# A written order on TensorE from the second query chunk to branch A, with attention handed out one step at a time

## The chip, the cores and the metric

The kernel runs on one core of a Trainium2 chip. The metric is the device time of one execution in microseconds (us). The median of three runs of the kernel before is 1961.41 us, the runs lie between 1960.43 and 1962.89 us.

## What is computed

The kernel is one decoder block on 256 tokens with 2048 channels. Two token mixers run beside each other, are merged with sigmoid gates, and a SwiGLU feed-forward network follows. The change touches mixer A (attention with three kinds of keys: compressed, selected blocks, window), the gate of mixer A and the matrix that takes mixer A's output. All of it is float32.

```
h = rms_norm(x); P = h @ W_in          # q | k,v for 3 branches | gates | GDN parts | merge gates mA, mB
o_A = attention(q, k, v, gates)        # 16 heads in 4 groups of 4; three softmaxes per head
o_B = gated_delta_net(...)
x   = x + (sigmoid(mA) * (o_A @ W_brA) + sigmoid(mB) * (o_B @ W_brB)) @ W_out
x   = x + (silu(h2 @ W_gate) * (h2 @ W_up)) @ W_down
```

## The kernel before

**Dense chunks.** Every projection is cut into chunks of 512 output columns. `chunk_tok` computes one chunk for both token tiles (two tiles of 128 tokens). The weights come in pairs of two blocks of 128 rows (`load_pair`): one DMA of 512 KB into `raw` (4 buffers), a copy on ScalarE that rounds it to the upper part `whi` (line 107), and a subtraction on VectorE that leaves the lower part `wlo` (line 108); each of these has 3 buffers. One pair feeds 12 matmuls of 512 columns: 2 blocks, 2 token tiles, and 3 products each (lines 122, 123, 124). A chunk with 2048 input rows has 8 pairs. It accumulates in two PSUM banks out of four (`psm`, tag `mm`), one per token tile, and its `evac` function then takes them.

**Side work.** `chunk_tok` is a generator that yields after each pair. `run` calls `pump` at each yield, and `pump` advances the generator at the head of the queue `side` by one step. Attention is such a generator: `attend(gi, t, ...)` for head group `gi` and token tile `t`. The two token tiles of one group are alternated by `zipped`, one step of each in turn. Small results use four other PSUM banks (`sps()`, tag `sd`).

**Attention.** `evac_q` normalizes a query chunk (`normed_T`: square, sum, power, multiplication into `nv`, which has two buffers) and transposes it on TensorE. `attend` then does, for each of four heads, the products with the keys, a maximum on VectorE (line 514) and the exponentials with their sums on ScalarE (line 517). Token tile 0 uses one bank per head, token tile 1 two. After the fourth head a factor per row is worked out (lines 552 to 556). Then the probabilities go segment by segment (three for token tile 0, five for token tile 1): a multiplication by the factor (line 580, or 564 for the compressed keys), four transposes (583, 572), a split into `ph` and `pl` on ScalarE and VectorE (176 and 177, or 573 and 574), and matmuls with the values (588 to 590, or 575). At the end the result is split into `oTA_hi` and `oTA_lo`.

**The order.** A planner puts the traced instructions of each engine into one fixed queue per engine: it walks through a modelled time and takes what is ready, earlier traced work first. Each engine then works through its queue in that order. The order of the trace is thus not the order on TensorE. Traced after the first query chunk are the chunks q1, q2, q3, the four chunks of merge gate A (`mA`), the first six pairs of each of the first two chunks of branch A (`run_pair(br[0], br[1], 2)`, which then drains the side work), and the rest of branch A. Branch A's blocks 12 to 15 need the output of the last head group. When the attention is through, its SBUF pool `nsa` is closed (`scr.__exit__`), and a pool `gdn` is opened on the same memory; `gdn_prep` of the second mixer then loads rows (`N`, `Q`, `eR`, from `grow_d`) by DMA from SyncE's queue and works on them with VectorE (lines 723 to 729) and ScalarE (731 to 737).

Of the kernel before, what the change touches and what calls it, by code (L numbers as in the profile page):

```python
# [2 lines left out]

# [17 lines left out]
KD = D // P  # L21
# [3 lines left out]
R = 4  # L25
# [7 lines left out]
C_Q = 0  # L33
# [5 lines left out]
C_MA = 13392  # L39
C_MB = 15440  # L40
# [3 lines left out]
def tile_hybrid_block(  # L44
# [22 lines left out]
    nc = tc.nc  # L67
    x = x[0]
    out = out[0]
    w_in = w_in[0]  # L70
    w_branch_a = w_branch_a[0]
# [17 lines left out]
    def nm(s):  # L89
        uid[0] += 1  # L90
        return f"{s}_{uid[0]}"
# [4 lines left out]
    def sps():  # L96
        return pss.tile([P, 512], F32, tag="sd", name=nm("sd"))
# [12 lines left out]
        )  # L110
        return hi, lo

    def chunk_tok(w, c0, width, kts, stat, evac):
        ps = [psm.tile([P, 512], F32, tag="mm", name=nm("mm")) for _ in range(NT)]
        for k0 in range(0, kts, 2):
            hi, lo = load_pair(w, k0, c0, width)
            for j in range(2):
                kt = k0 + j
                for t in range(NT):
                    sh, sl = stat(kt, t)  # L120
                    o = ps[t][:, :width]
                    nc.tensor.matmul(o, lhsT=sh, rhs=hi[:, j, :width], start=kt == 0, stop=False)  # L122
                    nc.tensor.matmul(o, lhsT=sh, rhs=lo[:, j, :width], start=False, stop=False)  # L123
                    nc.tensor.matmul(o, lhsT=sl, rhs=hi[:, j, :width], start=False, stop=kt == kts - 1)  # L124
            yield
        for t in range(NT):
            evac(t, ps[t])
        yield
# [19 lines left out]
    side = deque()  # L148

    def pump(n=1):  # L150
        for _ in range(n):
            if not side:
                return
            try:
                next(side[0])
            except StopIteration:
                side.popleft()

    def drain():
        while side:  # L160
            pump()

    def run(gen, n=1):
        for _ in gen:
            pump(n)

    def run_pair(ga, gb, n):

        for g in (ga, gb):
            for _ in range(6):  # L170
                next(g)
# [19 lines left out]
    ident = consts.tile([P, P], F32, name="ident")  # L191
# [44 lines left out]
    nsa = scr.__enter__()  # L236
# [151 lines left out]
        nc.scalar.activation(hi, src, AF.Copy, scale=gcol)  # L388
        nc.vector.scalar_tensor_tensor(lo, src, gcol, hi.bitcast(F32), ALU.mult, ALU.subtract)

    def normed_T(pst, hi, lo, gcol):

        sq = nsa.tile([P, 512], F32, tag="sq", name=nm("sq"), bufs=1)
        nc.scalar.activation(sq, pst, AF.Square)
        ss = nsa.tile([P, 4], F32, tag="ss", name=nm("ss"), bufs=4)
        nc.vector.tensor_reduce(ss, sq.rearrange("p (g d) -> p g d", g=4), AX.X, ALU.add)
        rs = nsa.tile([P, 4], F32, tag="rs", name=nm("rs"), bufs=4)
        rstd_of(ss, 1.0 / DH, EPS, rs)
        nv = nsa.tile([P, 512], F32, tag="nv", name=nm("nv"), bufs=2)
        nc.vector.tensor_tensor(  # L400
            nv.rearrange("p (g d) -> p g d", g=4),
            pst.rearrange("p (g d) -> p g d", g=4),
            rs.unsqueeze(2).to_broadcast([P, 4, P]),
            ALU.mult,
        )
        pt = sps()
        for i in range(4):
            nc.tensor.transpose(pt[:, i * P : (i + 1) * P], nv[:, i * P : (i + 1) * P], ident)
        gained(hi, lo, pt.rearrange("p (g d) -> p g d", g=4), gcol)
# [3 lines left out]
    def evac_kv(b, kind):  # L413
        def f(t, ps):
            if b == 0:
                tm = nsa.tile([P, 512], F32, tag="nv", name=nm("nv"), bufs=2)
                nc.scalar.activation(tm, ps, AF.Copy)
                if t == 0:
                    rawT[kind] = nsa.tile([P, G, S], F32, tag="rawT", name=nm("rawT"))
                pt = sps()  # L420
                for i in range(4):
                    nc.tensor.transpose(pt[:, i * P : (i + 1) * P], tm[:, i * P : (i + 1) * P], ident)
                nc.vector.tensor_copy(rawT[kind][:, :, t * P : (t + 1) * P], pt.rearrange("p (g c) -> p g c", g=4))
                if t == 1:
                    side.append(compress(kind))
            elif kind == 1:
                hilo(vh[b][:, t, :], vl[b][:, t, :], ps)
            else:
                o = KOFF[(b, t)]
                normed_T(ps, kTh[:, :, o : o + P], kTl[:, :, o : o + P], kg[:, b : b + 1])  # L430

        return f

# [56 lines left out]
    def evac_q(gi):  # L490
        both = {}

        def f(t, ps):
            qh = nsa.tile([P, R, P], F32R, tag="qh", name=nm("qh"), bufs=4)
            ql = nsa.tile([P, R, P], F32R, tag="ql", name=nm("ql"), bufs=4)
            normed_T(ps, qh, ql, qg)
            both[t] = attend(gi, t, qh, ql)
            if t == 1:
                side.append(zipped(both[0], both[1]))

        return f
# [2 lines left out]

        return bass.AP(tensor=pw.tensor, offset=pw.offset, ap=[list(pw.ap[0]), [144, 2], [1, 128]])

    def attend(gi, t, qh, ql):
        W = 272 if t == 0 else 528
        pb = nsa.tile([P, R, 528], F32, tag="pbuf", name=nm("pb"), bufs=2)
        nmx = nsa.tile([P, R, 3], F32, tag="nmx", name=nm("nmx"), bufs=2)  # L510
        sm = nsa.tile([P, R, 3], F32, tag="sm", name=nm("sm"), bufs=2)
# [45 lines left out]
            segs = [(0, 1, 0), (128, 2, 0), (256, 0, 0)]  # L557
        else:
            segs = [(0, 1, 1), (128, 1, 0), (256, 2, 0), (384, 0, 0), (400, 2, 1)]
        po = sps()  # L560
        for i, (c0, b, kt) in enumerate(segs):
            ph = nsa.tile([P, 512], F32R, tag="ph", name=nm("ph"), bufs=2)
            if b == 0:
                nc.vector.tensor_tensor(
                    cb.rearrange("p r (q c) -> p r q c", q=3)[:, :, :, :16],
                    pb[:, :, c0 : c0 + 16].unsqueeze(2).to_broadcast([P, R, 3, 16]),
                    f[:, :, 0].unsqueeze(2).unsqueeze(3).to_broadcast([P, R, 3, 16]),
                    ALU.mult,
                )
                pt = sps()  # L570
# [4 lines left out]
                nc.tensor.matmul(po, lhsT=vst[:, gi, :], rhs=ph[:96], start=i == 0, stop=i == len(segs) - 1)  # L575
                yield
                continue
            n = P
            seg = pb[:, :, c0 : c0 + n]
            nc.vector.tensor_tensor(seg, seg, f[:, :, b].unsqueeze(2).to_broadcast([P, R, n]), ALU.mult)  # L580
            pt = sps()
            for r in range(R):
                nc.tensor.transpose(pt[:n, r * P : (r + 1) * P], pb[:, r, c0 : c0 + n], ident)  # L583
            pl = nsa.tile([P, 512], F32R, tag="pl", name=nm("pl"), bufs=2)
            hilo(ph[:n], pl[:n], pt[:n])
            gs = slice(gi * P, (gi + 1) * P)
            wh, wl = vh[b][:, kt, gs], vl[b][:, kt, gs]
            nc.tensor.matmul(po, lhsT=wh, rhs=ph[:n], start=i == 0, stop=False)
            nc.tensor.matmul(po, lhsT=wh, rhs=pl[:n], start=False, stop=False)
            nc.tensor.matmul(po, lhsT=wl, rhs=ph[:n], start=False, stop=i == len(segs) - 1)  # L590
            yield
# [21 lines left out]
    side.append(narrow())  # L613
    for c in (5, 0, 1, 2, 4):
        run(chunk_tok(w_in, C_KV + c * 512, 512, KD, stat_h, evac_kv(c // 2, c % 2)), 1)
    for gi in range(4):
        run(chunk_tok(w_in, C_Q + gi * 512, 512, KD, stat_h, evac_q(gi)), 1)


    keep = {n: dram.tile([NT, P, D], F32, name=n, bufs=1) for n in ("mA_d", "mB_d", "brA_d")}  # L620
# [1 line left out]
    def evac_keep(n, c):  # L622
        def f(t, ps):
            st = stream.tile([P, 512], F32, tag="stg", name=nm("stg"), bufs=2)
            nc.scalar.activation(st, ps, AF.Copy)
            nc.sync.dma_start(keep[n][t, :, c * 512 : (c + 1) * 512], st)

        return f

    def chunk_m(n, c, r):  # L630
        run(chunk_tok(w_in, (C_MA if n == "mA_d" else C_MB) + c * 512, 512, KD, stat_h, evac_keep(n, c)), r)

    for c in range(4):
        chunk_m("mA_d", c, 1)

    def stat_of(hi, lo):
        def f(kt, t):
# [3 lines left out]
        return f  # L641

    stat_oa = stat_of(oTA_hi, oTA_lo)
    br = [chunk_tok(w_branch_a, c * 512, 512, KD, stat_oa, evac_keep("brA_d", c)) for c in range(4)]
    run_pair(br[0], br[1], 2)
    scr.__exit__(None, None, None)
    for g in br:
        run(g)
# [53 lines left out]
    for cg in range(4):  # L702
        for c in range(8):
            o = c * 32 + 8 * cg + c
# [434 lines left out]
```

## Time and profile before

| | before |
|---|---|
| median of 3 runs | 1961.41 us |
| the profiled execution's own time | 1961.53 us |
| its span, first to last instruction | 1959.8 us |
| TensorE busy | 1934.2 us (99%) |
| VectorE busy | 1157.1 us (59%) |
| ScalarE busy | 928.9 us (47%) |
| mean granted TensorE clock | 0.997 |

TensorE's matmuls overlap each other in the profile, so that a matmul of 512 columns is shown with some 0.39 us while the next one starts about 0.23 us after it. The busy share therefore hides small waits; starts of successive matmuls show them.

### The profile page before, as it was taken

The page shows a single profiled execution, that of the slowest core. Times are in us where ns is not written, and L with a number is a line of the kernel's source. Part 1 is how long each engine was busy: PE and PEld are TensorE (multiplying, and loading weights), DVE is VectorE, ACT ScalarE, POOL GpSimd, SP SyncE. Part 2 cuts the span into 40 slices and gives each one's busy share as a digit, 9 for nine tenths or more (in the row PEclk, how much of TensorE's full clock was granted, in tenths as well). Part 3 has the DMA queues.
Part 4 walks back from the last instruction along what each step waited for, and adds up shares of the span by engine and source line. Part 5 has one row for each costly group of instructions (what it writes and reads, how often), then busy time and mean ns, then how long its engine had stood idle before and what let it go on. Part 6 is the DMA issues. An engine that isn't in the chain of part 4 may idle for free.

```text
span 1959.8 us, 27239 instructions
## 1 busy us (share of the span) xinstructions
PE 1934.2 (99%) x10469; PEld 1651.3 (84%) x10469; DVE 1157.1 (59%) x1717; ACT 928.9 (47%) x1377; POOL 54.0 (3%) x98
## 2 busy tenths in 40 slices
PE   7999999999999999999999999999999999999999
PEld 6878888887998998999987788888888888888887
DVE  5555766665468677787774755555544544544443
ACT  5434555555454554654543544444444444443333
POOL 0001000001000000100100000000000000000000
PEclk9999999999999999999999999999999999999999
DMA  7566555547756666565564956666666666666664
GB/s 226 167 193 183 168 145 162 171 152 213 209 172 200 173 178 198 164 191 166 153 200 153 345 190 184 191 190 187 189 188 192 190 188 191 191 188 204 203 206 136
DMA packets 207845, 367.10 MB, mean 187 GB/s; under 512 B 25593, under 2 KB 34786, under 8 KB 207330
## 3 DMA queue, kind: packets, MB, share of 16 engines
q1 hardware_dynamic: 207682, 365.35, 62.5%
q8 instruction: 82, 1.34, 0.3%
q14 instruction: 49, 0.40, 0.1%
q10 hardware_dynamic: 32, 0.01, 0.0%
HBM read 355.76 MB, written 9.45 MB: 186 GB/s over the span
## 4 chain that ended last, share of the span: by engine, by line
PE 96%; DMA 2%; DVE 1%; ACT 0%; SPq 0%; issue 0%; POOL 0%; ACTq 0%; POOLq 0%; DVEq 0%
PE mm L123 24%; PE mm L124 24%; PE mm L122 24%; PE mm L141 4%; PE mm L143 4%; PE mm L142 4%; PE sd L183 1%; PE sd L689 1%; PE sd L452 1%; PE sd L769 1%; DMA raw<-in_w_branch_b_dram 1%; PE sd L583 1%; DMA raw<-in_w_branch_a_dram 0%; PE sd L269 0%; DMA xin<-in_x_dram 0%; DMA N<-grow_d 0%
## 5 line engine op out<-in xcount | busy, mean ns | idle before, releaser
L108 DVE TENSOR_TENSOR wlo<-raw,whi 128x1024 fp32r<-128x1024 f32 x632 | 774.1, 1226 | 650.5 <-ACT whi L107 648.6
L107 ACT ACTIVATE whi<-raw 128x1024 fp32r<-128x1024 f32 x632 | 669.5, 1060 | 810.6 <-PE mm L124 675.4
L123 PE MATMUL mm<-wlo,hT_hi 128*128 128x512 f32 x704 | 276.7, 393 | 0.0
L124 PE MATMUL mm<-whi,hT_lo 128*128 128x512 f32 x704 | 276.1, 392 | 0.0
L124 PE MATMUL mm<-whi,h2T_lo 128*128 128x512 f32 x704 | 274.0, 389 | 0.0
L123 PE MATMUL mm<-wlo,h2T_hi 128*128 128x512 f32 x704 | 273.9, 389 | 0.0
L122 PE MATMUL mm<-whi,hT_hi 128*128 128x512 f32 x704 | 260.3, 393 | 0.0
L122 PE MATMUL mm<-whi,h2T_hi 128*128 128x512 f32 x704 | 249.9, 390 | 0.0
L143 PE MATMUL mm<-hT_hi,wlo 128*128 128x256 f32 x768 | 218.4, 285 | 0.0
L141 PE MATMUL mm<-hT_hi,whi 128*128 128x256 f32 x768 | 218.4, 285 | 0.0
L142 PE MATMUL mm<-hT_lo,whi 128*128 128x256 f32 x768 | 218.3, 284 | 0.0
L123 PEld LDWEIGHTS mm<-wlo,hT_hi 128*128 128x128 f32 x704 | 132.2, 188 | 27.6 <-issue 1.1
L124 PEld LDWEIGHTS mm<-whi,h2T_lo 128*128 128x128 f32 x704 | 132.1, 188 | 27.5
L124 PEld LDWEIGHTS mm<-whi,hT_lo 128*128 128x128 f32 x704 | 132.3, 188 | 27.2 <-issue 0.4
L122 PEld LDWEIGHTS mm<-whi,h2T_hi 128*128 128x128 f32 x704 | 132.2, 188 | 27.1
L123 PEld LDWEIGHTS mm<-wlo,h2T_hi 128*128 128x128 f32 x704 | 132.2, 188 | 27.1
L122 PEld LDWEIGHTS mm<-whi,hT_hi 128*128 128x128 f32 x704 | 132.1, 188 | 26.4 <-issue 0.2
L141 PEld LDWEIGHTS mm<-hT_hi,whi 128*128 128x128 f32 x768 | 147.2, 192 | 0.6
L142 PEld LDWEIGHTS mm<-hT_lo,whi 128*128 128x128 f32 x768 | 147.2, 192 | 0.2
L143 PEld LDWEIGHTS mm<-hT_hi,wlo 128*128 128x128 f32 x768 | 146.9, 192 | 0.4
L124 PE MATMUL mm<-whi,act 128*128 128x512 f32 x352 | 136.9, 389 | 0.0
L123 PE MATMUL mm<-wlo,act 128*128 128x512 f32 x352 | 136.9, 389 | 0.0
(292 smaller groups left out, 2244.7 us busy)
## 6 DMA issues: line engine op xcount, KB each, us to landing
raw<-in_w_in_dram SPq DMA_DIRECT2D x272, 512.0 KB, 3.6
raw<-in_w_gate_dram SPq DMA_DIRECT2D x88, 512.0 KB, 4.3
raw<-in_w_up_dram SPq DMA_DIRECT2D x88, 512.0 KB, 3.6
raw<-in_w_down_dram SPq DMA_DIRECT2D x88, 512.0 KB, 4.6
raw<-in_w_branch_a_dram SPq DMA_DIRECT2D x32, 512.0 KB, 4.6
raw<-in_w_branch_b_dram SPq DMA_DIRECT2D x32, 512.0 KB, 5.6
raw<-in_w_out_dram SPq DMA_DIRECT2D x32, 512.0 KB, 4.1
wc<-in_w_cmp_dram SPq DMA_DIRECT2D x16, 256.0 KB, 3.9
```

The source lines that it names most:

```text
L107: nc.scalar.activation(hi[:, :, :width], raw[:, :, :width], AF.Copy)
L108: nc.vector.tensor_tensor(lo[:, :, :width], raw[:, :, :width], hi[:, :, :width].bitcast(F32), ALU.subtract)
L122: nc.tensor.matmul(o, lhsT=sh, rhs=hi[:, j, :width], start=kt == 0, stop=False)
L123: nc.tensor.matmul(o, lhsT=sh, rhs=lo[:, j, :width], start=False, stop=False)
L124: nc.tensor.matmul(o, lhsT=sl, rhs=hi[:, j, :width], start=False, stop=kt == kts - 1)
L141: nc.tensor.matmul(o, lhsT=hi[:, j, ws], rhs=xh[:, kt, :], start=first, stop=False, skip_group_check=True)
L142: nc.tensor.matmul(o, lhsT=hi[:, j, ws], rhs=xl[:, kt, :], start=False, stop=False, skip_group_check=True)
L143: nc.tensor.matmul(o, lhsT=lo[:, j, ws], rhs=xh[:, kt, :], start=False, stop=last, skip_group_check=True)
L183: nc.tensor.transpose(pt[:, i * P : (i + 1) * P], s4, ident)
L452: nc.tensor.matmul(pc[:60, :P], lhsT=kp[:, l0 + l, :], rhs=wc[:, l, :], start=l0 + l == 0, stop=l0 + l == 31)
L583: nc.tensor.transpose(pt[:n, r * P : (r + 1) * P], pb[:, r, c0 : c0 + n], ident)
L689: nc.tensor.transpose(pt[:, i * P : (i + 1) * P], src(i), ident)
```

## The change

`attend` now begins with the transposes of its own query (`turned`), which makes one step more; `evac` of a query chunk only normalizes (`normed`). In the second half of `attend` the segments are shifted against each other: a step issues the value matmuls of the segment before (`weigh(i - 1)`), then the transposes and the split of this one (`turn(i)`), then the multiplication for the next one (`scale(i + 1)`). `chunk_tok` can yield twice per pair (`fine`). The chunks q1 to q3, mA 0 to 3 and the first twelve half pairs of branch A's first two chunks are traced under `tc.manual_schedule` for TensorE, which keeps TensorE's instructions in the order in which they are traced; the queues of the other engines are still the planner's. `spread` hands out 0.62 attention steps per yield.

```diff
-    def chunk_tok(w, c0, width, kts, stat, evac):
+    def chunk_tok(w, c0, width, kts, stat, evac, fine=False):
...
                     nc.tensor.matmul(o, lhsT=sl, rhs=hi[:, j, :width], start=False, stop=kt == kts - 1)
+                if fine and j == 0:
+                    yield
             yield
...
-    def normed_T(pst, hi, lo, gcol):
+    def normed(pst):
...
+        return nv
+
+    def turned(nv, hi, lo, gcol):
+
         pt = sps()
...
         def f(t, ps):
-            qh = nsa.tile([P, R, P], F32R, tag="qh", name=nm("qh"), bufs=4)
-            ql = nsa.tile([P, R, P], F32R, tag="ql", name=nm("ql"), bufs=4)
-            normed_T(ps, qh, ql, qg)
-            both[t] = attend(gi, t, qh, ql)
+            both[t] = attend(gi, t, normed(ps))
...
-    def attend(gi, t, qh, ql):
-        W = 272 if t == 0 else 528
+    def attend(gi, t, nv):
+        qh = nsa.tile([P, R, P], F32R, tag="qh", name=nm("qh"), bufs=4)
+        ql = nsa.tile([P, R, P], F32R, tag="ql", name=nm("ql"), bufs=4)
+        turned(nv, qh, ql, qg)
+        yield
...
+        def turn(i):
+            c0, b, kt = segs[i]
+            pt = sps()
+            ph = nsa.tile([P, 512], F32R, tag="ph", name=nm("ph"), bufs=2)
...
+            hilo(ph, pl, pt)
+            return ph, pl
+
+        def weigh(i, ph, pl):
...
+        scale(0)
+        got = None
+        for i in range(n + 1):
+            if i:
+                if i == 1:
+                    po = sps()
+                weigh(i - 1, *got)
+            if i < n:
+                got = turn(i)
+                if i + 1 < n:
+                    scale(i + 1)
+                yield
...
-    for gi in range(4):
-        run(chunk_tok(w_in, C_Q + gi * 512, 512, KD, stat_h, evac_q(gi)), 1)
+    run(chunk_tok(w_in, C_Q, 512, KD, stat_h, evac_q(0)), 1)
...
-    for c in range(4):
-        chunk_m("mA_d", c, 1)
...
-    br = [chunk_tok(w_branch_a, c * 512, 512, KD, stat_oa, evac_keep("brA_d", c)) for c in range(4)]
-    run_pair(br[0], br[1], 2)
+    br = [chunk_tok(w_branch_a, c * 512, 512, KD, stat_oa, evac_keep("brA_d", c), fine=True) for c in range(4)]
+
+    def spread(gens, share):
+
+        due = 0.0
+        for g in gens:
+            for _ in g:
+                due += share
+                while due >= 1.0:
+                    pump()
+                    due -= 1.0
+
+    assert len(side) == 1
+    with tc.manual_schedule(engines={mybir.EngineType.PE}):
+        spread([chunk_tok(w_in, C_Q + gi * 512, 512, KD, stat_h, evac_q(gi), fine=True) for gi in (1, 2, 3)], 0.62)
+        spread([gen_m("mA_d", c, True) for c in range(4)], 0.62)
+        spread([islice(g, 12) for g in (br[0], br[1])], 0.62)
+        drain()
     scr.__exit__(None, None, None)
     for g in br:
         run(g)
```

## Rows read from the trace of the kernel before

**Rows 1.** The page: engine totals, and the two weight-splitting groups.
```profile
PE 1934.2 (99%) x10469; PEld 1651.3 (84%) x10469; DVE 1157.1 (59%) x1717; ACT 928.9 (47%) x1377; POOL 54.0 (3%) x98
...
L108 DVE TENSOR_TENSOR wlo<-raw,whi 128x1024 fp32r<-128x1024 f32 x632 | 774.1, 1226 | 650.5 <-ACT whi L107 648.6
L107 ACT ACTIVATE whi<-raw 128x1024 fp32r<-128x1024 f32 x632 | 669.5, 1060 | 810.6 <-PE mm L124 675.4
```

**Rows 2.** Windows: length, busy us (count) of PE, PEld, DVE, ACT, POOL; clock, DMA.
```profile
211.00:448.00 237.00, 237.00 (x1208) 197.00 (x1207) 156.27 (x268) 137.14 (x317) 6.05 (x6) 1.00 0.53 156
448.00:480.00 32.00, 28.05 (x111) 20.75 (x109) 19.75 (x47) 16.89 (x24) 6.72 (x38) 0.95 0.82 215
480.00:512.00 32.00, 32.00 (x146) 26.62 (x145) 14.71 (x12) 14.07 (x17) 0.00 (x0) 1.00 0.75 229
```

**Rows 3.** Timeline of TensorE, 185 to 320 us: start, duration, engine, line, operation.
```profile
221.63 0.39 PE L123 MATMUL mm<-wlo,hT_hi 128*128 128x512 f32 x1
...
224.35 0.39 PE L123 MATMUL mm<-wlo,hT_hi 128*128 128x512 f32 x1
224.58 0.28 PE L521 MATMUL sd<-kTh,qh 128*128 128x256 f32 x1
...
225.48 0.38 PE L521 MATMUL sd<-kTh,qh 128*128 128x272 f32 x1
...
225.98 0.37 PE L521 MATMUL sd<-kTh,qh 128*128 128x256 f32 x1
```

**Rows 4.** Waits of TensorE, 440 to 480 us: total, times, longest.
```profile
PE mm L123 <- DVE wlo L108: 2.5, 2, 2.3
...
PE mm L122 <- ACT oTA_hi L176: 0.7, 1, 0.7
```

**Rows 5.** Timeline of all engines, 443 to 481 us; in brackets idle time, releaser.
```profile
453.55 0.40 PE L590 MATMUL sd<-ph,vl 128*128 128x512 f32 x1
...
454.06 0.32 POOL L695 MEMSET p<- 128x256 f32 x1 [161.80 <-PE sd L590]
...
454.63 0.51 PE L122 MATMUL mm<-whi,oTA_hi 128*128 128x512 f32 x1 [0.69 <-ACT oTA_hi L176]
...
457.76 0.20 ACT L736 ACTIVATE esc<-esc 128x4 f32<-128x4 f32 x1 [3.18 <-DVE esc L723]
...
460.39 0.73 PE L122 MATMUL mm<-whi,oTA_hi 128*128 128x512 f32 x2 [0.69 <-ACT whi L107]
...
463.40 0.68 PE L123 MATMUL mm<-wlo,oTA_hi 128*128 128x512 f32 x1 [2.28 <-DVE wlo L108]
...
463.94 0.63 ACT L737 ACTIVATE eR<-eR 128x512 f32<-128x512 f32 x1 [3.61 <-DMA eR<-grow_d]
...
464.48 1.04 ACT L107 ACTIVATE whi<-raw 128x1024 fp32r<-128x1024 f32 x1
...
466.44 0.63 PE L122 MATMUL mm<-whi,oTA_hi 128*128 128x512 f32 x1
```

**Rows 6.** Timeline of all engines, 416 to 426.5 us.
```profile
416.94 0.29 PE L529 MATMUL sd<-mask,identb 128*128 128x272 bf16 x1
...
419.94 1.29 DVE L580 TENSOR_TENSOR pb<-pb,fac 128x512 f32<-128x512 f32 x2
...
422.24 0.24 PE L543 MATMUL sd<-mask,identb 128*128 128x144 bf16 x1
...
424.76 1.90 DVE L580 TENSOR_TENSOR pb<-pb,fac 128x512 f32<-128x512 f32 x3
```

**Rows 7.** Timeline of all engines, 436.5 to 439 us.
```profile
436.76 0.60 PE L583 MATMUL sd<-ident,pb 128*128 128x128 f32 x4
...
438.03 0.69 DVE L177 TENSOR_TENSOR pl<-sd,ph 128x512 fp32r<-128x512 f32 x1 [1.73 <-ACT ph L176]
```

**Rows 8.** Timeline of all engines, 386.9 to 390.6 us.
```profile
387.89 0.60 PE L583 MATMUL sd<-ident,pb 128*128 128x128 f32 x4
...
390.07 0.69 DVE L177 TENSOR_TENSOR pl<-sd,ph 128x512 fp32r<-128x512 f32 x1
```

More of the change, by code (lines that the diff above doesn't have):

```diff
@@ L2 @@
 from contextlib import ExitStack
+from itertools import islice
 import concourse.bass as bass
@@ L429, in f @@
                 o = KOFF[(b, t)]
-                normed_T(ps, kTh[:, :, o : o + P], kTl[:, :, o : o + P], kg[:, b : b + 1])
+                turned(normed(ps), kTh[:, :, o : o + P], kTl[:, :, o : o + P], kg[:, b : b + 1])
         return f
@@ L559, in attend, with scale @@
             segs = [(0, 1, 1), (128, 1, 0), (256, 2, 0), (384, 0, 0), (400, 2, 1)]
-        po = sps()
-        for i, (c0, b, kt) in enumerate(segs):
-            ph = nsa.tile([P, 512], F32R, tag="ph", name=nm("ph"), bufs=2)
+        n = len(segs)
+        def scale(i):
+            c0, b, kt = segs[i]
             if b == 0:
@@ L569, in attend @@
                 )
-                pt = sps()
+            else:
+                seg = pb[:, :, c0 : c0 + P]
+                nc.vector.tensor_tensor(seg, seg, f[:, :, b].unsqueeze(2).to_broadcast([P, R, P]), ALU.mult)
+        def turn(i):
+            c0, b, kt = segs[i]
+            pt = sps()
+            ph = nsa.tile([P, 512], F32R, tag="ph", name=nm("ph"), bufs=2)
+            if b == 0:
                 for r in range(R):
@@ L574, in attend @@
                 nc.vector.tensor_tensor(ph[32:64], pt[32:64], ph[32:64].bitcast(F32), ALU.subtract)
[L575 to L581, printed above, removed]
+                return ph, None
             for r in range(R):
-                nc.tensor.transpose(pt[:n, r * P : (r + 1) * P], pb[:, r, c0 : c0 + n], ident)
+                nc.tensor.transpose(pt[:, r * P : (r + 1) * P], pb[:, r, c0 : c0 + P], ident)
             pl = nsa.tile([P, 512], F32R, tag="pl", name=nm("pl"), bufs=2)
-            hilo(ph[:n], pl[:n], pt[:n])
+            hilo(ph, pl, pt)
+            return ph, pl
+        def weigh(i, ph, pl):
+            c0, b, kt = segs[i]
+            if b == 0:
+                nc.tensor.matmul(po, lhsT=vst[:, gi, :], rhs=ph[:96], start=i == 0, stop=i == n - 1)
+                return
             gs = slice(gi * P, (gi + 1) * P)
             wh, wl = vh[b][:, kt, gs], vl[b][:, kt, gs]
[L588 to L591, printed above, removed]
+            nc.tensor.matmul(po, lhsT=wh, rhs=ph, start=i == 0, stop=False)
+            nc.tensor.matmul(po, lhsT=wh, rhs=pl, start=False, stop=False)
+            nc.tensor.matmul(po, lhsT=wl, rhs=ph, start=False, stop=i == n - 1)
+        scale(0)
[10 more added lines that the diff above has]
+                yield
         ts = slice(t * P, (t + 1) * P)
@@ L628, in evac_keep, with gen_m @@
         return f
+    def gen_m(n, c, fine=False):
+        return chunk_tok(w_in, (C_MA if n == "mA_d" else C_MB) + c * 512, 512, KD, stat_h, evac_keep(n, c), fine)
     def chunk_m(n, c, r):
-        run(chunk_tok(w_in, (C_MA if n == "mA_d" else C_MB) + c * 512, 512, KD, stat_h, evac_keep(n, c)), r)
-    for c in range(4):
-        chunk_m("mA_d", c, 1)
+        run(gen_m(n, c), r)
     def stat_of(hi, lo):
```

## The prediction

> **What bounds the kernel now.** The page comes first: TensorE is busy for 99% of the span, the other engines far less [rows 1], so only time in which TensorE does not take its next matmul can be won. Busy time cannot show that, because matmuls overlap in it. So the pitch comes next: between two starts of line 123 lie 12 matmuls and 2.72 us, 0.2267 us each [rows 3]. Then the windows over the stretch that the change touches, from the end of the first query chunk (211 us) to the end of branch A (512 us). From 211 to 448 the busy time of TensorE fills the window [rows 2], and the view of its waits between 205 and 440 us has no row. From 480 to 512 it is full again. Only 448 to 480 is not: 28.05 us busy, clock 0.95, 111 matmuls, four of which are transposes that began before 448 and end there. The other 107 have 512 columns and need 107 x 0.2267 = 24.3 us. They took 32 us less some 0.2 us for the transposes' end and 0.1 us for the change of kind. **About 7.4 us are lost there**, and nowhere else in the stretch.
>
> What they are is in the waits and the timeline. First, the tail of the attention: the last value matmul starts at 453.55, the first matmul that needs its result at 454.63 [rows 5], 1.08 us instead of 0.23; the planner had nothing else ready. Second, a starved weight path. When the attention ends, the second mixer's pool opens (GpSimd's first memset waits for that very matmul), and its preparation gets into the queues of ScalarE and VectorE between the splits of the weights. ScalarE stands 3.18 us before `esc` and 3.61 us before `eR`, both waiting in the end for a DMA, while `whi` stands behind; TensorE gets weights at 460.39 and, after 2.28 us without work, at 463.40 [rows 4, 5]. Third, the clock: from 463.40 to 466.44 lie seven matmuls at 0.434 us, against 0.2267; the granted clock of the window, 0.95, shows the fall to the lower level [rows 2, 5]. About eight matmuls at 0.2 us too much are 1.65 us. The first part is about 0.9 us, with small delays before it 1.4; the rest, some 6 us, is the starved path and its clock.
>
> **The change, part by part.** All matmuls, transposes, copies and DMAs are issued as often as before; the work on TensorE is the same, so the sum is what the 7.4 us become, and which new waits the written order makes.
>
> *Where the attention ends.* A half step is 6 matmuls, 1.36 us. A chunk gives 16 half steps and 17 yields. A head group needs 20 steps (9 for token tile 0, 11 for token tile 1) and one empty call, four groups 84, of which one is done before the written part. The three calls of `spread` may hand out 31, 42 and 14 (0.62 of 51, 68 and 24 yields). So the last step of the attention falls on half step 3 of branch A's second chunk, and nine half steps (12.2 us) of other work still stand before the first matmul that needs the last group. The first loss, 1.4 us, is gone.
>
> *The starved path (cost D).* The pool still opens when the last step is through, and the same preparation, with its ten DMAs, still enters both queues. What changes is the lead. Before, TensorE's prepared weights at 454.63 lasted for some 4.5 us, 1.7 pairs, because the blocks that waited for the last group held all three weight buffers. With dense work at hand the three buffers are full, two to three pairs, 2.5 in the mean. That is 0.8 pairs, 2.2 us, more against a starvation of 6 us; and if no single wait is as long as 2.28 us, the 1.65 us of the clock fall away too. I take 6.0 - 2.2 - 1.65 = **2.1 us** that remain, between 0 (the planner puts the splits first) and 4.2 (the clock falls again).
>
> *Splits that are one step old (cost A).* The value matmuls of a segment now stand at a fixed place, one step of their token tile later. While both tiles alternate, that is two steps, at least 4 us, and the split needs 1.36 us from the last transpose to the end of `pl` (437.36 to 438.72) [rows 7] or, with a weight split ahead on VectorE, 2.27 us (388.49 to 390.76) [rows 8]: covered. Token tile 1 has two steps more than tile 0; there its steps follow one another. I count the yields: of these eight places, four have two half steps between (2.72 us, covered) and four only one, 1.36 us. Each of the four waits 0 to 0.9 us; with 0.45 that is **1.8 us** (0 to 3.6). Nothing else can run on TensorE meanwhile.
>
> *The first transposes after the softmax (cost B).* They stand behind the maximum, three exponentials, the factor and `scale(0)`. In the trace this took 3.4 us from the end of the last mask matmul to the end of the first multiplication for token tile 0 (417.23 to 420.6) and 3.0 us for tile 1 (422.48 to 425.4) [rows 6]. With the key products of a step at 0.9 us for tile 1 and 0.5 us for tile 0 [rows 3], the written order leaves these gaps, counted in yields: tile 0: 5.0, 5.0, 3.6, 3.6 us for the four groups; tile 1: 3.2, 4.5, 3.2, 3.2 us (for the first, two half steps and the 0.45 us of tile 0's transposes). With a chain of 3.7 us, a little above the rows, as weight splits lie between, the waits are 0.2 + 1.4 = about **1.5 us**; at the rows' own 3.0 and 3.4 us they are nothing, and with one whole weight split more (1.06 us [rows 1], so a chain of up to 4.5 us) 3.9 us.
>
> *A bank (cost C).* `nv` has two buffers, and a query now stays in `nv` until its group's first step. The third chunk's normalization waits for the step of group 2 that comes one half step into the second mA chunk. Its two banks are thus not free when that chunk starts, and it must take those that the chunk before it has just filled, behind a copy of 128x512 (some 0.6 us for such a copy: in [rows 7] the one ahead of the subtraction lies between 437.36 and 438.03). Half of this lies under the other tile's matmuls: **0.5 us**, from 0 to 1.1.
>
> *The clock after short waits.* The rows show that about 0.85 us without a matmul at 454 us did not lower the clock (it fell only after the 2.28 us), so waits of the kind above cost their length and no more. The Trainium skill, page "TensorE: Matmul & The Clock Gate", section "A second HAM failure mode: psum-queue depth-cycling", says that small idle times between groups of matmuls can make the clock swing between its two levels; by that rule each wait would cost more than its length. The trace so far doesn't bear it out.
>
> Sum: 2.1 + 1.8 + 1.5 + 0.5 = 5.9 us of 7.4 us are given back: **-1.5 us**. The profiled execution took 1961.53 us (a span of 1959.8 and 1.7 us around it), 0.12 us over the median, so it is 1961.41 - 1.5 = **1959.9 us**.
>
> **The rivals.** 0.2% is 3.9 us, about what a measurement of this kernel can tell from no change.
> (1) *The covers hold.* The planner knows the written order, traces the attention's work ahead of the weights and fits it in; A and B come to 1 us together, D to 1, C to 0.3. Result -5.1 us, 1956.3. For it: VectorE and ScalarE are free for 34% and 42% of 211 to 448 us [rows 2], and TensorE had no wait there. Against it: that order was chosen by readiness.
> (2) *The other side: the preparation starves the weights as before.* If ScalarE's queue holds `whi` behind `eR` for the whole 10 us between 454.06 and 464.48 [rows 5], TensorE needs 3.7 pairs in that time and has 2.5 to 3; it waits some 2 to 3 us and loses the clock, 4.2 us, and a second round for the next group adds up to 2 more, so that only 1.4 us of the 7.4 are won. With A to C at their middle, 3.8, this is +2.4 us; the kernel is slower by over 0.2% once A to C exceed 5.3 us: at their upper ends (8.6) it is +7.2 us, 1968.6.
> (3) *The clock swings.* If each of about ten waits lowers the clock as at 463.40, that is 10 x 1.65 = 16 us, 1976. The page named above speaks for it, the pitch after 454 us against it.
> (4) *The change does nothing*: the planner's order is like the written one, with the same tail. The steps make this unlikely, as the tail moves by nine half steps.
>
> **How the numbers follow.** The forecast's case has 0.42, the covers that hold 0.33, the starved path 0.15, the clock 0.05, no effect 0.05. Of the forecast's case 0.04 may fall under -3.9 us; of the starved path's, a third (0.05) stays within 3.9 us. So faster is 0.33 + 0.04 = 0.37, same 0.38 + 0.05 + 0.05 = 0.48, slower 0.10 + 0.05 = 0.15. The likeliest case alone has 1957 to 1963. The range for 8 in 10 goes from 1954.4 (nearly all 7.4 us won) to 1966.5 (the second rival half way).
>
> **What would show it.** Right: no wait of TensorE for `oTA_hi`; the first memset of the second mixer's pool some 12 us before branch A's first matmul on block 12; short waits of the value matmuls at the end of a group; a wait for `whi` or `wlo` after the pool opens that is shorter than 2.28 us. Wrong: TensorE's waits for `scale` or `ph` sum to over 5 us, or the clock falls in several places; or the planner orders the second mixer and branch B differently, which this sum leaves out: branch B has a similar stretch that could move by some us either way.

## The result, and the profile after

The changed kernel takes 1983.99 us, the median of four runs (1981.6 to 1987.55), beside 1961.33 us before: a ratio of 1.0116 (95% interval 1.0102 to 1.013), so 22.7 us slower. The forecast was 1959.9 us, its range ended at 1966.5 us. The profiled execution took 1981.6 us with a span of 1979.9 us, 20.1 us over that of before; it is the fastest of the four, and what makes the median 2.4 us longer than it is in no trace.

All of the 20.1 us arise where the order was written. The last matmul of branch A starts at 510.95 us before and at 531.03 us after, 20.1 us later; the last of branch B then comes at 1155.46 us instead of 1135.37, the last of the feed-forward network at 1975.07 instead of 1955.00, still 20.1 us. TensorE's busy total, 1934.2 us in [rows 1], is now 1939.4 us, and its share fell from 99% to 98%.

The windows of the changed kernel, with the columns of [rows 2]. The stretch from 211 to 448 us, which was full, now has 11.5 us in which no matmul runs, and the one from 448 to 480 lost still more than before.

```profile
211.00:448.00 237.00, 225.50 (x1125) 184.83 (x1124) 150.18 (x260) 132.23 (x309) 6.53 (x6) 0.99 0.47 140
448.00:480.00 32.00, 26.53 (x109) 20.51 (x108) 17.89 (x46) 12.73 (x17) 4.33 (x37) 0.89 0.68 191
```

The waits of TensorE between 205 and 440 us, where before has no row at all. Line 593 is the transposes of a segment, line 580 the multiplication (`scale`) ahead of them, 415 the transposes of a query, 601 the value matmul of the compressed keys. The second row names `whi`, which the transposes don't read; by the program what they wait for there is `scale` as well.

```profile
PE sd L593 <- DVE pb L580: 8.4, 3, 4.1
PE sd L593 <- ACT whi L108: 1.9, 2, 1.2
PE sd L415 <- DVE nv L403: 1.4, 1, 1.4
PE sd L601 <- DVE ph L590: 1.2, 2, 0.6
PE sd L415 <- DVE ss L384: 1.0, 1, 1.0
```

And between 440 and 535 us, the answer to [rows 4]: no wait for `oTA_hi`, a longer one for `wlo`.

```profile
PE mm L124 <- DVE wlo L109: 4.9, 2, 4.4
PE sd L601 <- DVE ph L590: 0.6, 1, 0.6
```

Waits leave out the time in which a late matmul gets going, so the account is made from starts. From 200 us to branch A's last matmul, each distance between two starts is taken less the pitch of its kind (0.227 us for 512 columns, 0.109 to 0.125 for 128 to 272 columns, 0.04 for the mask products). Distances over it by 0.5 us are put down to the matmul that came late; 512-column pitches near 0.427 us, where the granted clock is 0.50, the lower of its two levels, to the clock. What is left over is the last row but one.

| lost on TensorE, us (places) | before | after |
|---|---|---|
| first transposes after the softmax (cost B) | 0 | 11.1 (5) |
| transposes of the first group's query | 0 | 2.7 (2) |
| value matmuls of the compressed keys (cost A) | 0 | 2.3 (3) |
| weights not ready (cost D) | 3.3 (2) | 5.2 (2) |
| the tail, for `oTA_hi` | 0.9 (1) | 0 |
| 512-column matmuls at the lower clock | 1.4 (7) | 4.2 (21) |
| all smaller distances | 8.0 | 9.2 |
| sum | 13.5 | 34.7 |

The sum rose by 21.2 us; the changed kernel came to this stretch 1.1 us earlier, which gives the 20.1 us.

What cost B looks like is seen in the timeline of head group 1, token tile 1 (TensorE, then VectorE, then ScalarE). The last product with the keys (its mask) ends at 297.07 us, the first transposes start at 305.08.

```profile
296.83 0.24 PE L550 MATMUL sd<-mask,identb 128*128 128x144 bf16 x1
...
301.32 0.39 PE L125 MATMUL mm<-whi,hT_lo 128*128 128x512 f32 x1
305.08 0.99 PE L593 MATMUL sd<-ident,pb 128*128 128x128 f32 x4 [3.37 <-DVE pb L580]
...
297.12 1.22 DVE L109 TENSOR_TENSOR wlo<-raw,whi 128x1024 fp32r<-128x1024 f32 x1
...
298.53 0.83 DVE L521 TENSOR_REDUCE nmx<-sd 128x1 f32<-128x256 f32 x3
299.27 0.68 DVE L399 TENSOR_REDUCE ss<-sq 128x4 f32<-128x512 f32 x1
299.87 1.22 DVE L109 TENSOR_TENSOR wlo<-raw,whi 128x1024 fp32r<-128x1024 f32 x1
301.00 0.68 DVE L180 TENSOR_TENSOR pl<-sd,ph 128x512 fp32r<-128x512 f32 x1
...
301.82 0.69 DVE L399 TENSOR_REDUCE ss<-sq 128x4 f32<-128x512 f32 x1
302.42 0.22 DVE L560 RECIPROCAL fac<-fac 128x12 f32<-128x12 f32 x1
302.83 1.23 DVE L109 TENSOR_TENSOR wlo<-raw,whi 128x1024 fp32r<-128x1024 f32 x1 [0.19 <-ACT whi L108]
...
304.24 1.89 DVE L580 TENSOR_TENSOR pb<-pb,fac 128x512 f32<-128x512 f32 x3
...
297.84 0.60 ACT L397 ACTIVATE sq<-mm 128x512 f32<-128x512 f32 x1 [1.82 <-PE mm L125]
...
300.03 0.47 ACT L524 ACTIVATE pb<-sd,nmx 128x256 f32<-128x256 f32 x1
...
301.18 0.61 ACT L397 ACTIVATE sq<-mm 128x512 f32<-128x512 f32 x1
```

The chain itself is the maximum (521), the exponentials (524), the factor (560) and `scale` (580). In VectorE's queue stand between and before them three weight splits, a split of another tile (180) and the sums of squares of the next query chunk (399), which ScalarE's squares (397) must bring first. VectorE is busy for all but 0.9 us of the time to the end of the first multiplication: TensorE is not waiting for one late result but for a queue to be worked off. From the last mask product to the end of the first multiplication are 7.9 us, instead of the 3.0 us that [rows 6] show for the last head group.

### The profile page after: what moved, and what is told of

Same layout as the page of the kernel before. It is cut to its first block, busy times and chain, and to the rows that moved or that the text cites. A ratio compares the mean times of both kernels' runs of the same rounds, so it can differ in the third digit from the quotient of the medians.

```text
span 1979.9 us, 27247 instructions
## 1 busy us (share of the span) xinstructions
PE 1939.4 (98%) x10469; PEld 1653.4 (84%) x10469; DVE 1159.0 (59%) x1717; ACT 932.1 (47%) x1377; POOL 53.3 (3%) x98
## 4 chain that ended last, share of the span: by engine, by line
PE 94%; DMA 2%; DVE 2%; ACT 1%; SPq 0%; issue 0%; POOL 0%; ACTq 0%; POOLq 0%; DVEq 0%
PE mm L124 24%; PE mm L123 24%; PE mm L125 24%; PE mm L144 4%; PE mm L146 4%; PE mm L145 4%; PE sd L186 1%; PE sd L734 1%; PE sd L459 1%; DMA Q<-grow_d 1%; PE sd L814 1%; DVE wlo L109 1%; DMA raw<-in_w_branch_b_dram 1%; ACT whi L108 1%; PE sd L593 1%; PE sd L272 0%
## 5 line engine op out<-in xcount | busy, mean ns | idle before, releaser
L123 PE MATMUL mm<-whi,hT_hi 128*128 128x512 f32 x704 | 268.4, 401 | 0.0
```

## The experiments

Theory 1: the time is lost in the written order's own waits. It has two forms: (1a) the chain to the first transposes is long where the next query chunk's normalization falls into it; (1b) it is long everywhere. The rival, theory 2, is the weight path that the second mixer's preparation starves. All ratios are to the kernel before, run in the same job.

**Planned order, same steps.** The written order is taken away, all else stays.

```diff
-    with tc.manual_schedule(engines={mybir.EngineType.PE}):
+    with ExitStack():
```


> The changed kernel with the same steps, the same half-pair yields and the same share of 0.62, but without the written order: the planner orders TensorE again. Theory 1 (the loss is TensorE standing in a fixed order before the first transposes after a softmax, whose chain sits in the queues of VectorE and ScalarE behind other work; 11.1 us of waits and some 3.6 us of lowered clock): these waits go, and the time falls from 1984 to between 1956 and 1964 us. Rival (the finer steps and the reordered segments themselves cost, by more changes of kind on TensorE and more side work per stretch, whoever orders TensorE): it stays at 1976 us or more.

1960.44 us, ratio 0.9994 (0.9984 to 1.0003). The finer steps, the shifted segments and the moved transposes cost nothing where the planner orders them; TensorE then waits only for weights (3.6 us). The whole loss belongs to the written order: theory 1.

**One step more between softmax and transposes**, and a share that keeps the end in place.

```diff
         scale(0)
+        yield
...
-        spread([gen_m("mA_d", c, True) for c in range(4)], 0.62)
+        spread([gen_m("mA_d", c, True) for c in range(4)], 0.70)
...
```


> The changed kernel with one more step (a yield) between the first multiplication by the factor and the first transposes, in both token tiles, and a share of 0.70 in place of 0.62 so that the eight more steps still fit before branch A's second half. Theory 1: the chain after the softmax gets two more turns, some 5 us, beside the 3.2 to 5 us it had, against chains of 4 to 8 us in the trace; the waits of the first transposes fall from 11.1 us to under 2 us and the two falls of the clock go: about 1984 - 13 = 1971 us. Rival (the chain is late because VectorE and ScalarE have too much to do in this stretch; a longer distance only moves the wait to the next step): 1980 us or more.

1972.88 us, 1.0054 (1.0039 to 1.0069): 11.1 us won; the share alone won 4.7 (next experiment). The waits of line 593 are gone altogether. The two longest of TensorE's waits between 205 and 535 us are now for weights, all after 449 us:

```profile
PE mm L123 <- ACT whi L108: 4.7, 1, 4.7
PE mm L124 <- DVE wlo L109: 4.7, 2, 3.0
```

**The share alone**, in all three calls, without the new step.

```diff
-        spread([gen_m("mA_d", c, True) for c in range(4)], 0.62)
+        spread([gen_m("mA_d", c, True) for c in range(4)], 0.70)
...
```


> The changed kernel with a share of 0.70 in place of 0.62 and nothing else. By counting yields, the first transposes of token tile 1 then no longer fall just behind the end of a query chunk in groups 0 and 1, but in the middle of a chunk, or before its end; every gap gets a little shorter (1.43 half steps a turn in place of 1.61). Theory 1a (the two long waits, 4.3 and 3.5 us, come from the normalization of the next query chunk, which stands inside the softmax chain on VectorE): they fall to some 1.5 us, and the clock no longer falls there: 1984 - 8 = 1976 us. Theory 1b (the chain is long anyway, the normalization is by chance beside it): shorter gaps make longer waits, 1984 to 1990 us.

1979.29 us, 1.0088 (1.0073 to 1.0103): neither form as forecast. The first long wait stays (3.2 us; the normalization still stands in that chain), the second falls to 0.96 us, and the waits of line 593 are 7.5 us in total. Which chains meet the normalization changes with the share; one of the two still did.

**Five steps ahead**, the share as it was.

```diff
+    pump(5)
     with tc.manual_schedule(engines={mybir.EngineType.PE}):
```


> The changed kernel in which five steps of the attention are issued ahead of the written part, so that all later steps fall eight half steps earlier in the chunks; gaps and share stay. The first transposes of groups 0 and 1 then fall into the middle of a query chunk, away from its normalization. Theory 1a (the normalization inside the softmax chain makes the two long waits): they fall from 4.1 and 3.4 to some 1.5 us, and the two falls of the clock go: 1984 to 1975 us. Theory 1b (the chain is as long anywhere): 1982 us or more.

1972.83 us, 1.006 (1.0047 to 1.0074). The attention runs ahead of the normalization, and only two waits of line 593 are left, 2.5 us in total, the longest 1.3. Head group 1, token tile 1 again:

```profile
285.61 0.24 PE L550 MATMUL sd<-mask,identb 128*128 128x144 bf16 x1
...
291.70 0.63 PE L593 MATMUL sd<-ident,pb 128*128 128x128 f32 x4 [1.24 <-ACT whi L108]
```

From mask product to the end of the first multiplication, the chain of token tile 1 takes 5.8, 5.7, 4.2 and 4.2 us here for the four groups, and 7.2, 7.9, 4.8 and 4.2 us in the changed kernel. TensorE's work in between is as long as before in group 1 (4.5 us), so there the shorter chain alone shortens the wait, from 3.37 to 1.24 us: 1a holds for the long waits. In group 0 the place gave one half step more as well (4.45 us of work instead of 3.1), so its wait fell for both reasons. But 1b is right in part: without any normalization in it the chain still takes 4.2 to 5.8 us, behind the weight splits and the subtraction of the other token tile.

**Rows not loaded.** `N`, `Q` and `eR` of the first two head groups are filled with a constant by GpSimd, so their decay factors are not the true ones.

```diff
+        if hg < 2:
+            for v in (st.N, st.Q, st.eR):
+                nc.gpsimd.memset(v, -3000.0)
+        else:
...
```


> The changed kernel in which the rows of the second mixer's first two head groups are not loaded by DMA but filled with a constant by GpSimd; that leaves out ten DMAs of these rows, and the decay factors of these groups are then not the true ones, while all the work on VectorE, ScalarE and TensorE stays. Theory 2 (the starvation of 466 to 479 us comes from ScalarE and VectorE waiting in order for these DMAs): about 7 us go, 1984 to 1977 us. Rival (the preparation's own work on the two engines starves the weight splits): at most 2 us go.

1979.61 us, 1.0083 (1.0066 to 1.01), 4.4 us won. Two waits for `wlo` are left, 1.76 and 1.82 us: VectorE's work on the rows still stands between the splits, and six of its instructions took 5.33 us beside GpSimd's filling, so the run is confounded. By starts the waits for weights fell from 5.2 to 3.9 us, and the fall of the clock behind them (1.6 us) is gone; how much of the rest is the filling stays open here.

**Preparation behind the splits**, in the kernel before and in the changed one. The VectorE and ScalarE work of `gdn_prep` is ordered behind the newest weight split; the ten loads stay where they were.

```diff
+    def behind(after, inst):
+        tc.add_manual_dep(
+            inst.ins, after.name,
+            mybir.DependencyInfo(mybir.DependencyClass.NoSync, mybir.DependencyReason.DATA),
+            reason="behind a weight pair",
+        )
...
-        nc.scalar.activation(st.N, st.N, AF.Exp, scale=-1.0)
+        behind(na, nc.scalar.activation(st.N, st.N, AF.Exp, scale=-1.0))
...
```


> The kernel before with one thing changed: the work of the second mixer's preparation on VectorE and ScalarE (the factors esc, N, Q, eR of a head group) is put behind the newest weight split traced ahead of it on the same engine, by an ordering edge without a semaphore; the loads stay where they are. Theory 2 (from 458 to 476 us TensorE starves because these instructions stand, waiting for their DMAs, in front of weight splits): the starvation and the lowered clock, some 6 us, go: 1961 to 1955 us. Rival (the splits are late because all three weight buffers were held by blocks that waited for the last head group): 0 to 2 us go.

> The changed kernel with the same edge for the preparation. Theory 2: the 7.3 us between 466 and 480 us go, 1984 to 1977 us. Rival (the preparation's place has nothing to do with it, the written order itself is late there): within 2 us of 1984.

Before: 1959.79 us, 0.9991 (0.9982 to 1.0), only 1.4 us won, at the edge of the noise. After: 1978.48 us, 1.009 (1.0076 to 1.0104), 5.5 us won in the median; the profiled execution, 1982.11 us, is the slowest of the four and shows no gain up to branch A's end. In the first, one wait of 4.5 us for `whi` takes the place of the shorter ones, with nothing of the preparation in the queues of ScalarE and VectorE; ScalarE stands there for 9.2 us before a copy that waits for an earlier store of branch A's result. Its stretch up to branch A's end is 1.7 us longer than in the kernel before. What it won lies later: 1.9 us between branch A's last matmul and branch B's first, 0.5 us within branch B.

**The written order mended**: the new step and the share 0.70, the preparation behind the splits, and the first group's first step three half steps after its query chunk.

```diff
-    run(chunk_tok(w_in, C_Q, 512, KD, stat_h, evac_q(0)), 1)
+    for i, _ in enumerate(chunk_tok(w_in, C_Q, 512, KD, stat_h, evac_q(0))):
+        if i < 8:
+            pump()
...
         scale(0)
+        yield
...
-    def spread(gens, share):
+    def spread(gens, share, due=0.0):
...
-        spread([gen_m("mA_d", c, True) for c in range(4)], 0.62)
+        spread([gen_m("mA_d", c, True) for c in range(4)], 0.70)
...
```


> The written order with what the runs so far point to: one more step between the softmax and the first transposes, a share of 0.70, the preparation's work behind the weight splits, and the first group's first step three half steps after its query chunk rather than at its end. If the waits found so far are all there is (11.1 + 3.6 for the first transposes and their clock, 7.3 for the preparation, 2.7 at the start): 1984 - 24 = 1960 us, the kernel before's time. If the written order costs elsewhere too: 1965 us or more.

1965.97 us, 1.0024 (1.0015 to 1.0034). 18 of 22.7 us are back, less than forecast; TensorE has one long wait, 5.5 us for `whi`, and the transposes at the start wait no more. Here the cause can be read, since VectorE and ScalarE are idle beside it. SyncE's queue and ScalarE in the timeline of this run:

```profile
447.55 1.71 SPq L102 DMA_DIRECT2D raw<-in_w_branch_a_dram  x1
449.31 1.98 SPq L778 DMA_DIRECT2D eR<-grow_d  x1
...
457.25 1.25 SPq L778 DMA_DIRECT2D eR<-grow_d  x1
458.60 13.19 SPq L102 DMA_DIRECT2D raw<-in_w_branch_a_dram  x5
...
469.08 1.06 ACT L108 ACTIVATE whi<-raw 128x1024 fp32r<-128x1024 f32 x1 [9.45 <-DMA raw<-in_w_branch_a_dram]
```

and its DMA issues by what they load (number, KB each, median us from issue to landing), between 440 and 475 us; the last row is the same for 400 to 440 us:

```profile
raw<-in_w_branch_a_dram SPq DMA_DIRECT2D x10, 512.0 KB, 9.2
N<-grow_d SPq DMA_DIRECT2D x4, 256.0 KB, 9.6
...
raw<-in_w_branch_a_dram SPq DMA_DIRECT2D x11, 512.0 KB, 3.8
```

The six loads of rows from 449 to 458.5 us stand ahead of the weights in the queue, and ScalarE gets the first weights behind them 10.5 us after their issue. So the loads are what is left of this wait, whatever the engines do.

**Loads of rows spaced.** Each of the ten goes behind another of the last sixteen weight loads of branch A. This was tried on the mended order, on the kernel before, and on the planned order of the first experiment, each with the preparation behind the splits.

```diff
+    slots = loads[-16:]
+
+    def row_load(hg, out, in_):
+        d = nc.sync.dma_start(out, in_)
+        if hg < 2:
+            behind(slots.pop(0), d)
...
-        nc.sync.dma_start(st.eR, rows(1))
+        row_load(hg, st.eR, rows(1))
```


> The mended written order with one thing more: the ten loads of decay rows N, Q and eR of the first two head groups are put on SyncE's queue one at a time, each behind another of the last sixteen weight loads of branch A, where they stood together. Theory (what is left of the starved path is the loads: ten of 256 KB at once stand ahead of the weight loads, whose data then comes 10 us after its issue where 3.8 us are usual): no wait for weights over 1 us between 440 and 520 us, no fall of the clock there, 5.7 + 1.6 us less, so 1958.7 us (1957 to 1961). Rival (splits on ScalarE and VectorE or the bandwidth itself hold the weights): within 2 us of the 1966.0 us of the mended order. A second rival: the rows come too late for the preparation, and the second mixer starts some us late.

> The kernel before, with its preparation behind the weight splits and the ten loads of rows spaced over the last sixteen weight loads in the same way; TensorE's order stays the planner's. Theory: the wait for weights of 4.9 us and its fall of the clock go, so 1961.2 - 1.4 - 6.5 = 1953.3 us (1952 to 1956). Rival: within 2 us of 1959.8 us, the time without the spacing.

> The changed kernel's steps and emission without the written order (TensorE planned), with the same late preparation and spaced rows. Theory: the steps cost nothing, the weights come in time, so 1960.4 - 4 - 1.7 = 1954.7 us (1953 to 1957). Rival: 1959 to 1961, as the planner's order has waits of its own that the loads don't set.

Mended: 1956.81 us, 0.9977 (0.9968 to 0.9987). Before: 1951.33 us, 0.9951 (0.9938 to 0.9963). Planned steps: 1949.14 us, 0.9941 (0.9929 to 0.9954), the fastest of all and faster than both kernels of this study. Each won more than forecast (9.2, 8.5 and 11.3 us beside the same kernel without the spacing, in the third without the deferred preparation too). The spacing without the deferral was not run, so whether the deferral is needed is not shown. The mended written order is still 7.7 us slower than the planned steps with the same treatment. In the third TensorE has no wait from 205 to 545 us; its window that answers to the second of [rows 2]:

```profile
448.00:480.00 32.00, 32.00 (x142) 26.41 (x141) 15.01 (x15) 15.52 (x18) 3.23 (x36) 1.00 0.89 285
```

Branch A ends at 502.96 us instead of 510.95. Of the 13.0 us between the two profiled executions the rest comes later, 1.9 us before branch B's first matmul, as with the deferral alone, and 3.2 us within branch B; that part was not taken apart.

**The written order alone**: the changed kernel with deferred preparation and spaced loads, against the third of these.

> The changed kernel, written order and all, with the late preparation and the spaced loads of rows; beside the same steps in the planner's order (1949.1 us, no wait of TensorE from 205 to 545 us) it is the cost of the written order alone, with the weights in time in both. Theory 1 (the written order costs what its waits show: the first transposes 11.1 us and 3.6 us of clock behind them, the value matmuls 2.3 us, the first group's start 2.7 us, more changes of kind about 1.5 us): 1949.1 + 21 = 1970 us (1968 to 1972), no wait for weights after 440 us. Rival (with the loads out of the way the starved path and the written order's waits prove to share time): under 1966 us, or over 1974 us.

1970.7 us, 1.0053 (1.0039 to 1.0066), as theory 1 forecast, and no wait for weights after 440 us. Its waits of TensorE, 205 to 545 us (line 605 is 593, 592 is 580, 613 is 601 of the changed kernel), beside the same two of the first group's query, 1.0 and 1.4 us:

```profile
PE sd L605 <- DVE pb L592: 8.3, 3, 4.1
PE sd L605 <- ACT whi L108: 1.9, 2, 1.2
PE sd L613 <- DVE ph L602: 1.9, 3, 0.6
...
```

So the written order costs 21.6 us by itself with the weights in time in both. By starts, the two differ by 21.5 us up to branch A's end: 11.1, 2.7 and 2.3 us for the three kinds of waits, 2.8 us for the clock, and 2.6 us in small distances.

## Why the prediction was wrong

*What bounds the kernel.* Right: the loss of before was the starved stretch. With it mended, in the planned steps, TensorE's waits there are nothing, and branch A ends 8.0 us earlier where 7.4 us were counted (6.3 us in the kernel before itself, which keeps its tail).

*Cost B, the step that failed.* "With a chain of 3.7 us, a little above the rows": 1.5 us, at most 3.9 (from its own gaps and chains these come out at 1.7 and 4.3). Measured are 11.1 us and two falls of the clock behind the two longest waits, some 2.6 us more. The gaps between softmax and transposes were counted rightly (3.2 and 4.5 us for the two); the chain was not. Its 3.0 and 3.4 us came from the last head group [rows 6], at 417 to 425 us, when no query chunk is being normalized any more. For the first two groups the written order lets the next query's normalization fall into the chain of token tile 1, which then takes 7.2 and 7.9 us and gives 7.8 of the 11.1 us. The bound allowed one more weight split; in the second chain three stand. In the last two groups, with no normalization, the chains that wait take 4.2 to 4.8 us and give the other 3.3 us. The run with five steps ahead shows the part of the normalization: away from it the chain of group 1 is 2.2 us shorter, and the long waits go. The run with one more step shows that a longer cover does it as well.

The trace of before had such chains too. Token tile 1 took 10.3 and 7.8 us in its first two groups (232.78 to 243.10 and 301.41 to 309.17) and 3.0 us in the other two. The planner put other ready work in front of the transposes, so that no wait shows there. The second of them, from its last mask product to its multiplications:

```profile
301.17 0.24 PE L543 MATMUL sd<-mask,identb 128*128 128x144 bf16 x1
...
308.48 2.50 DVE L580 TENSOR_TENSOR pb<-pb,fac 128x512 f32<-128x512 f32 x4
```

*The start, not in the sum.* The first group's query transposes had been ready work for the planner; written, they stand where their normalization isn't through: 2.7 us. The prediction took the transposes' move for one step more and gave it no price.

*Cost A.* 1.8 us forecast at four places, 2.3 us measured, three places of 0.78 us. Right.

*Cost C.* No wait for a bank stands in the trace; whether one hides in the small distances was not tried.

*Cost D.* 2.1 us forecast, 6.8 us measured (5.2 and 1.6 of clock, against 4.7 before by the same count). The lead was there, as counted: the pool opened at 457 us and TensorE worked on to 466. But a lead of some pairs does not help against the thing that was taken for a detail, the ten loads. In the changed kernel (SyncE, ScalarE, VectorE, TensorE):

```profile
467.48 2.05 SPq L766 DMA_DIRECT2D eR<-grow_d  x1
469.63 7.32 SPq L102 DMA_DIRECT2D raw<-in_w_branch_a_dram  x3
...
468.28 0.63 ACT L782 ACTIVATE eR<-eR 128x512 f32<-128x512 f32 x1 [1.25 <-DMA eR<-grow_d]
...
471.66 1.03 DVE L774 TENSOR_SCALAR Q<-Q,gcum 128x128 f32<-128x128 f32 x4 [1.55 <-DMA Q<-grow_d]
...
473.81 1.22 DVE L109 TENSOR_TENSOR wlo<-raw,whi 128x1024 fp32r<-128x1024 f32 x1
...
475.08 0.80 PE L124 MATMUL mm<-wlo,oTA_hi 128*128 128x512 f32 x1 [4.44 <-DVE wlo L109]
```

VectorE waits for rows and holds `wlo` behind them; [rows 5] had shown ScalarE waiting for the same loads. Deferring the engines' work alone won 1.4 us in the kernel before, and none of it in this stretch; the loads stood ahead of the weights as before. That both suspects had to be mended is argued from this trace, not shown: the spacing alone was not run.

*The tail.* 1.4 us, gone as forecast (0.9 us by the count of starts).

*The clock.* In the profiled execution it fell three times, after waits of 4.08, 3.37 and 4.44 us; the three other waits of line 593, 0.69 to 1.22 us, left the pitch at 0.227, and in the run without loads of rows two of 1.76 and 1.82 us did too. Yet short waits are not safe. The two waits of the first group's query transposes stand in seven runs, and in four of them (one more step, rows not loaded, preparation behind the splits of the changed kernel, five steps ahead) the clock fell right behind them. In the run with one more step:

```profile
206.72 0.63 PE L415 MATMUL sd<-ident,nv 128*128 128x128 f32 x4 [0.98 <-DVE ss L384]
208.75 1.11 PE L415 MATMUL sd<-ident,nv 128*128 128x128 f32 x4 [1.40 <-DVE nv L403]
...
210.09 0.63 PE L124 MATMUL mm<-wlo,hT_hi 128*128 128x512 f32 x1
```

Its granted clock from 209 to 212 us is 0.50, the changed kernel's in the same place 1.00. The Trainium skill (page "TensorE: Matmul & The Clock Gate", section "A second HAM failure mode: psum-queue depth-cycling") reports a kernel whose clock swings with small idle times between groups of matmuls. These four falls agree with it; the waits of 0.69 to 1.82 us named first, which did not lower the clock, do not. The rival built on it, 1976 us, came nearest to the time, but by another mechanism: its falls were to cost 16 us, and the measured ones cost 4.2 us.

*The rivals.* The second, a preparation that starves as before, was right for cost D, and its price for A to C was still far too low. None let the chain between softmax and transposes cost more than the bound of cost B.

## What to carry to other kernels

A written order on one engine must leave room for the longest form of each chain that runs through the other engines' in-order queues: count what else is due there in that stretch (here the next chunk's normalization and three weight splits), and don't take the chain's length from a stretch where that work is over. A chain that no engine waits for today may already be long in the trace. A step's cover is best tested by moving it (one more yield, five steps ahead) rather than by counting gaps. Where a starved engine has several suspects in line, an edit to one of them may show little while another stands; here spacing ten 256 KB loads among the weight loads won 8.5 us in the kernel before once the engines' work had been put behind the splits.

## What the runs showed of the hardware

In the mended order's trace, weight loads of 512 KB land 3.8 us after their issue in the median from 400 to 440 us, and 9.2 us from 440 to 475 us, beside ten loads of rows of 256 KB whose medians are 9.1 to 9.8 us. SyncE needs up to 1.98 us to issue one of these instead of 0.34. The median alone doesn't tell whether TensorE starves: it is 6.1 us in the kernel before, with the loads of rows together (450 to 480 us), and 6.1 us in the planned steps with them spaced (450 to 490 us), where no wait came of it. Nor does the slowest weight load from 440 to 500 us fall much by the spacing, from 10.9 to 8.2 us in the mended order and from 8.7 to 8.2 us in the kernel before. What the spacing also changes is the place in SyncE's queue, which the six loads of rows held from 449.3 to 458.6 us; which of the two counts is not separated.

By the Trainium skill (page "DMA: Bandwidth & Descriptors", section "Issuing engines are not separate DMA queues") transfers started from several engines share the same 16 DMA engines, and issuing from several of them saves only the sequencer's time to start a transfer, usually small beside the transfer. Here the six loads of rows kept SyncE for 9.3 us; whether another issuing engine would have done as well as the spacing was not tried.

The length of a wait alone does not say whether the clock falls. Besides the pairs of 0.98 and 1.40 us above, in the run with one step more a wait of 3.04 us left the pitch as it was, as the timeline of TensorE shows; in the kernel before it had fallen after one of 2.28 us [rows 5], which itself came 3 us after one of 0.69. What decides it is not shown.

```profile
452.54 0.50 PE L124 MATMUL mm<-wlo,oTA_hi 128*128 128x512 f32 x1 [3.04 <-DVE wlo L109]
...
453.33 0.40 PE L124 MATMUL mm<-wlo,oTA_hi 128*128 128x512 f32 x1
453.57 0.39 PE L125 MATMUL mm<-whi,oTA_lo 128*128 128x512 f32 x1
```

In the changed kernel, after the wait of 4.08 us, the clock did not fall at once: the transposes and two matmuls still ran at the full pitch, and from 240.68 us seven at 0.427 us.

```profile
239.38 0.63 PE L593 MATMUL sd<-ident,pb 128*128 128x128 f32 x4 [4.08 <-DVE pb L580]
239.76 0.47 PE L123 MATMUL mm<-whi,hT_hi 128*128 128x512 f32 x1
...
240.68 0.63 PE L123 MATMUL mm<-whi,hT_hi 128*128 128x512 f32 x1
...
243.67 0.45 PE L124 MATMUL mm<-wlo,hT_hi 128*128 128x512 f32 x1
```
